# Eleven blocks of a transformer layer's weights by seven products of quarters, woven with the query/key tiles

## The chip, the core and the metric

The kernel runs on one core of one Trainium2 chip. The time is the device time of one execution, in microseconds (us). Engines are named as in the profile: PE is TensorE (PEld its weight loads), DVE is VectorE, ACT is ScalarE, POOL is GpSimd, SP is SyncE, which here only issues DMAs.

## What is computed

One layer on x of 256 tokens × 2048, in float32: a mixer with two branches, then a feed-forward block with a convolution over tokens. Each ends in a layer norm.

```
parts = x @ w_in                       # 2048 -> 9*1024 | 1024 1024 2048 2048 16 2048 2048
a_parts -> q, k, v of three dilated attention groups, 8 heads of 128
gq, gk, gv, gr, g_low, m_a, m_b = the rest
ya = (attention over the three groups) @ w_proj_a
o  = gated linear attention(gq, gk, gv, log_sigmoid(g_low @ gla_gate_w + b)/16)   # 4 heads, chunks of 64
yb = (rmsnorm(o) * silu(gr)) @ w_proj_b
y  = (sigmoid(m_a) * ya + sigmoid(m_b) * yb) @ w_out
x  = layernorm(alpha * x + y)
x  = layernorm(alpha * x + (silu(conv3(x @ w_gate)) * (x @ w_up)) @ w_down)
```

## The kernel before

All weights come as *pieces* of 128 partitions × 2048 float32 (1 MB), one DMA each on SP's queue, in the order of use. A piece is split in two parts that a single-pass matmul takes: `hi`, an ACT copy to float32r (L115), and `lo`, what is left, a DVE subtraction (L116). A product is then hi·hi + hi·lo + lo·hi. x is transposed and split in the same way, once (`X`, 16 blocks of 128 rows by 256 tokens, hi and lo side by side).

There are two forms of product. A *tile* (`b_tile`, L185 and L187) makes 128 output columns for all tokens, transposed: 16 matmuls of 512 with hi and 16 of 256 with lo. It serves q and k of the attention (48 tiles), gq and gk (16, `gqk`), gate and up of the feed-forward block (88, `fg` and `fu`). A *chunk* (`a_chunk`, L238 to L240) makes 512 output columns, with tokens on partitions: per piece 4 blocks of rows × 2 halves of tokens × 3 matmuls of 512, so 24 matmuls. It serves v, gv, gr, m, and the projections yp, pb, wo and wd.

The stages follow each other: v and q/k with the attention, gqk, gv, gr, then m, yp and pb in turn, wo, layer norm, the feed-forward block in parts of 20, 20 and 4 blocks (`FSPLIT`), the last norm. Small steps of attention and of the gated linear attention (GLA) are put in a list, `side`; `pump` takes one from it after a piece or a tile, so they stand between the products. One head of GLA is a chain: `gate` (pz, L483, then a log-sigmoid on ACT and DVE, L484 to L489), `decay` (a scan on DVE, L491, and exponentials), `keys` (q and k times these, L511, L517), `att` (ten small matmuls, L541, an ACT copy, a triangular mask on POOL, L549) and `outs` (pgo, L558 and L560, plain float32 matmuls, a root mean square and the output `o`, L567). Its four heads run beside the gv products.

Everything of the mixer stays in SBUF, in 38 buffers of 128x512 (`blk`). There are three buffers of raw pieces, two each of hi and lo, and 4 + 4 PSUM banks. The program's text is only a start for the order: a scheduler places the instructions of each engine, and the order on each engine is then fixed.

Of the kernel before, what the change touches and what calls it, by code (L numbers as in the profile page):

```python
# [20 lines left out]
NH = 8  # L21
# [14 lines left out]
FSPLIT = (20, 20, 4)  # L36
# [21 lines left out]
def hybrid_layer(ctx: ExitStack, tc: tile.TileContext, wp, xt, wgl, gw, par, relb, onehot, rows, xk, out):  # L58
    nc = tc.nc
    cpool = ctx.enter_context(tc.tile_pool(name="cpool", bufs=1))  # L60
    wpool = ctx.enter_context(tc.tile_pool(name="wpool", bufs=2))
    bpool = ctx.enter_context(tc.tile_pool(name="bpool", bufs=1))
    tpool = ctx.enter_context(tc.tile_pool(name="tpool", bufs=2))
    psm = ctx.enter_context(tc.tile_pool(name="psm", bufs=4, space=bass.MemoryType.PSUM))
    psx = ctx.enter_context(tc.tile_pool(name="psx", bufs=4, space=bass.MemoryType.PSUM))
    dpool = ctx.enter_context(tc.tile_pool(name="dpool", bufs=1, space=bass.MemoryType.DRAM))

# [11 lines left out]
    def blk(name, dt=F32):  # L79

        n_blk[0] += 1
        return bpool.tile([P, 512], dt, tag="blk", name=f"{name}_{n_blk[0]}", bufs=NBLK)

    def tmp(name, dt=F32):

        n_blk[0] += 1
        return tpool.tile([P, S], dt, tag="tmp", name=f"{name}_{n_blk[0]}", bufs=NTMP)

    def big(name, shape, dt=F32):

        n_blk[0] += 1
        return tpool.tile([P, *shape], dt, tag="big", name=f"{name}_{n_blk[0]}", bufs=7)

    def few(name, n, bufs=4):
        n_blk[0] += 1
        return tpool.tile([P, n], F32, tag=name, name=f"{name}_{n_blk[0]}", bufs=bufs)
# [15 lines left out]
    n_piece = [0]  # L112

    def split(hi, lo, src, engine=nc.vector):
        nc.scalar.activation(hi, src, AF.Copy)  # L115
        engine.tensor_tensor(lo, src, hi.bitcast(F32), op=ALU.subtract)  # L116

    def piece_in_blocks(i, on_pool=None):

        ws = []  # L120
        if on_pool is not None:
            raws = wpool.tile([P, 2048], F32, tag="raw", name=f"raw_{i}", bufs=3)
            nc.sync.dma_start(raws, wp[i])
        for c in range(4):
            cols = slice(c * 512, (c + 1) * 512)
            if on_pool is None:
                raw = blk("braw")
                nc.sync.dma_start(raw, wp[i, :, cols])
            else:
                raw = raws[:, cols]  # L130
            ws.append((blk("bhi", F32R), blk("blo", F32R)))
            split(*ws[-1], raw, nc.gpsimd if c in (on_pool or ()) else nc.vector)
        return ws

    def piece(before=(None,)):

        i = n_piece[0]
        n_piece[0] += 1
        raw = wpool.tile([P, 2048], F32, tag="raw", name=f"raw_{i}", bufs=3)
        hi = wpool.tile([P, 2048], F32R, tag="whi", name=f"whi_{i}")  # L140
        lo = wpool.tile([P, 2048], F32R, tag="wlo", name=f"wlo_{i}")
# [21 lines left out]
    def xtiles(name):  # L163
        return [bpool.tile([P, 4, 512], F32R, tag="xhl", name=f"{name}_{j}", bufs=4) for j in range(4)]

    X = xtiles("x")

    def load_x(j):
        def f():
            xr = blk("xraw")  # L170
            nc.sync.dma_start(xr, xt[:, j * 512 : (j + 1) * 512])
            k = slice(2 * (j % 2), 2 * (j % 2) + 2)
            xv = xr.rearrange("p (k t) -> p k t", k=2)
            split(X[j // 2][:, k, :S], X[j // 2][:, k, S:], xv)
        return f

# [13 lines left out]
    def b16(name, opnd, cuts=1):  # L190
        hi, lo = piece((None,) * cuts)
# [20 lines left out]
    def halves(a):  # L212
        return a.rearrange("p (a c) -> p a c", a=2)
# [557 lines left out]


NBLK = 38
NTMP = 12

# [114 lines left out]
```

## Time and profile before

| what | value |
|---|---|
| median of 3 runs | 1894.65 us (1894.32 to 1896.28) |
| the profiled execution's own time | 1894.34 us |
| span of that execution | 1892.5 us |
| PE / DVE / ACT / POOL busy | 99% / 58% / 46% / 4% |
| mean granted clock of PE | 0.997 |
| moved by DMA | 359.04 MB, 190 GB/s |

The span goes from the first to the last instruction that the profile shows; what lies outside it is start and end. Busy times of PE overlap a little, since matmuls are pipelined: how long a row of matmuls takes is read from the starts. The view of stages gives, for each stretch of the span, busy time and instruction count of PE, PEld, DVE, ACT and POOL, then the granted clock, the share of the 16 DMA engines and GB/s. In a timeline a row is start, duration, engine, line, operation, output and inputs, and in brackets the idle time before it and what ended that.

### The profile page before, as it was taken

How to read it: one execution, taken by the hardware profiler on the slowest of the kernel's cores; microseconds unless marked ns; L12 is line 12 of the kernel's file. 1: busy time of each engine (PE TensorE's matmuls, PEld its weight loads, DVE VectorE, ACT ScalarE, POOL GpSimd, SP SyncE). 2: the span in 40 equal slices, each digit the busy share in tenths (PEclk: the TensorE clock that was granted, in tenths of full speed). 3: DMA queues.
4: the chain of work that ended last, by engine and by line, in shares of the span. 5: the costliest groups of instructions: out<-in, count | busy, mean ns of one | idle time of the engine just before them, and what ended most of it. 6: DMA issues, size and time to landing. Idle time of an engine off the chain costs nothing.

```text
span 1892.5 us, 22845 instructions
## 1 busy us (share of the span) xinstructions
PE 1868.8 (99%) x9510; PEld 1585.6 (84%) x9510; DVE 1098.2 (58%) x1135; ACT 864.2 (46%) x936; POOL 81.0 (4%) x115
## 2 busy tenths in 40 slices
PE   8999999999999999999999999999999999999996
PEld 6888888888877788888888887888888888888885
DVE  5566475665655455445454557766644566664567
ACT  5445445454446544343434435555533455553342
POOL 0000000001000000000000003400000000000001
PEclk9999999999999999999999999999999999999998
DMA  8655545455534455555556654855555655555551
GB/s 283 237 178 180 193 167 193 172 189 181 182 137 155 150 184 181 197 193 187 198 182 219 236 195 145 242 203 190 191 180 198 245 185 194 184 194 185 215 200 67
DMA packets 57618, 359.04 MB, mean 190 GB/s; under 512 B 7089, under 2 KB 8012, under 8 KB 16940
## 3 DMA queue, kind: packets, MB, share of 16 engines
q1 hardware_dynamic: 52908, 345.10, 51.4%
q0 software_dynamic: 4464, 12.24, 2.5%
q8 instruction: 74, 1.21, 0.3%
q10 hardware_dynamic: 144, 0.26, 0.0%
q14 instruction: 28, 0.23, 0.0%
HBM read 355.41 MB, written 3.31 MB: 190 GB/s over the span
## 4 chain that ended last, share of the span: by engine, by line
PE 97%; DVE 2%; ACT 0%; issue 0%; DMA 0%; SPq 0%; ACTq 0%; DVEq 0%
PE qk L185 9%; PE fu L185 8%; PE fg L185 8%; PE qk L187 5%; PE fu L187 4%; PE fg L187 4%; PE wd_t L239 4%; PE wd_t L238 4%; PE wd_t L240 4%; PE gqk L185 3%; PE m_t L239 3%; PE m_t L240 3%; PE m_t L238 3%; PE v_t L238 2%; PE v_t L239 2%; PE v_t L240 2%
## 5 line engine op out<-in xcount | busy, mean ns | idle before, releaser
L116 DVE TENSOR_TENSOR wlo<-raw,whi 128x2048 fp32r<-128x2048 f32 (+1 forms) x336 | 738.8, 2201 | 662.3 <-ACT whi L115 645.7
L115 ACT ACTIVATE whi<-raw 128x2048 fp32r<-128x2048 f32 (+1 forms) x336 | 616.7, 1837 | 560.8 <-PE wd_t L240 107.9
L185 PE MATMUL qk<-x,whi 128*128 128x512 f32 x768 | 184.2, 392 | 0.0
L185 PEld LDWEIGHTS qk<-x,whi 128*128 128x128 f32 x768 | 140.9, 188 | 28.0
L185 PE MATMUL fu<-x,whi 128*128 128x512 f32 x688 | 164.3, 391 | 0.0
L185 PE MATMUL fg<-x,whi 128*128 128x512 f32 x672 | 160.2, 391 | 0.0
L185 PEld LDWEIGHTS fu<-x,whi 128*128 128x128 f32 x688 | 126.4, 188 | 24.5
L185 PEld LDWEIGHTS fg<-x,whi 128*128 128x128 f32 x672 | 123.6, 188 | 24.0
L238 PE MATMUL wd_t<-whi,h 128*128 128x512 f32 x344 | 133.9, 389 | 0.0
L239 PE MATMUL wd_t<-wlo,h 128*128 128x512 f32 x344 | 133.9, 389 | 0.0
L240 PE MATMUL wd_t<-whi,h 128*128 128x512 f32 x344 | 133.8, 389 | 0.0
L187 PEld LDWEIGHTS qk<-x,wlo 128*128 128x128 f32 x768 | 98.5, 191 | 3.8
L238 PE MATMUL m_t<-whi,x 128*128 128x512 f32 x256 | 99.9, 390 | 0.0
L187 PE MATMUL qk<-x,wlo 128*128 128x256 f32 x768 | 99.7, 283 | 0.0
L240 PE MATMUL m_t<-whi,x 128*128 128x512 f32 x256 | 99.6, 389 | 0.0
L239 PE MATMUL m_t<-wlo,x 128*128 128x512 f32 x256 | 99.6, 389 | 0.0
L187 PEld LDWEIGHTS fu<-x,wlo 128*128 128x128 f32 x688 | 88.2, 191 | 3.4
L187 PE MATMUL fu<-x,wlo 128*128 128x256 f32 x688 | 89.2, 283 | 0.0
L187 PEld LDWEIGHTS fg<-x,wlo 128*128 128x128 f32 x672 | 86.2, 191 | 3.3
L187 PE MATMUL fg<-x,wlo 128*128 128x256 f32 x672 | 87.2, 283 | 0.0
L238 PE MATMUL v_t<-whi,x 128*128 128x512 f32 x192 | 75.6, 396 | 1.7 <-ACT whi L115 1.7
L238 PEld LDWEIGHTS wd_t<-whi,h 128*128 128x128 f32 x344 | 64.6, 188 | 13.4
(229 smaller groups left out, 2717.7 us busy)
## 6 DMA issues: line engine op xcount, KB each, us to landing
raw<-in_wp SPq DMA_DIRECT2D x317, 1024.0 KB, 4.8
row<-in_rows POOLq DMA_DIRECT2D x24, 256.0 KB, 5.3
raw<-in_wp SPq DMA_DIRECT2D x20, 256.0 KB, 5.7
bias<-bvd POOLq DMA_DIRECT2D x32, 96.0 KB, 2.8
xraw<-in_xt SPq DMA_DIRECT2D x8, 256.0 KB, 5.7
r<-in_xk POOLq DMA_DIRECT2D x8, 256.0 KB, 5.3
braw<-in_wp SPq DMA_DIRECT2D x8, 256.0 KB, 6.0
out<-r SPq DMA_DIRECT2D x7, 256.0 KB, 2.5
```

The source lines that it names most:

```text
L115: nc.scalar.activation(hi, src, AF.Copy)
L116: engine.tensor_tensor(lo, src, hi.bitcast(F32), op=ALU.subtract)
L185: nc.tensor.matmul(ps, parts(kc)[0], opnd(kc), start=(kc == 0), stop=False)
L187: nc.tensor.matmul(ps[:, S:], parts(kc)[1], opnd(kc)[:, :S], start=False, stop=(kc == nk - 1))
L238: nc.tensor.matmul(ps, xh, hi, start=first, stop=False)
L239: nc.tensor.matmul(ps, xh, lo, start=False, stop=False)
L240: nc.tensor.matmul(ps, xl, hi, start=False, stop=last)
```

## The change

Eleven blocks of 2048 rows × 1024 columns (three of v, four of m, two of gv, two of gr) are no longer made by chunks. x and the block are cut in quarters, x by halves of tokens and of rows, the block by halves of rows and of columns; seven products of quarters (the form of Strassen and Winograd) give the four quarters of the result. `combine` makes four combinations of x once, on DVE. `seven` is one block, in seven steps: each product has two pieces of 12 matmuls. Four sums of weight pieces per block are made by DVE in place (`add`), four by a DMA on POOL's queue that adds into its destination (`add_by_dma`); five sums of results are made on DVE.

```
def part(ps, a, raw, p, first):
    hi, lo = two_parts(raw)
    for w, which in ((hi, 0), (hi, 1), (lo, 0)):
        for k in range(4): matmul(ps, a(4 * p + k)[which], w[:, k * 512 : (k + 1) * 512])
...
def add(a, b):
    tt(a, a, b, op=ALU.add)
def add_by_dma(a, b):
    nc.gpsimd.dma_start(a, b, accum_op=ALU.add)
...
def p1():      T = pieces 0, 1                     A = x11 T;  s = copy of A
def p5():      B12 = pieces 2, 3;  add(T, B12)     D = z T
def p67(p):    b = piece 4 + p;  add(T[p], b)      B += s2 T[p]
               add_by_dma(B12[p], b)               E += s3 B12[p]
               if p: s += B;  u = s + E;  store(1, 1, D - u)
def p3():      D += s4 B22;                        store(0, 1, D - s)
def p4():      B21 = pieces 6, 7;  add_by_dma(T, B21)   E = x22 T;  u += E;  store(1, 0, u)
def p2():      A += x12 B21;                       store(0, 0, copy of A)
```

(From `p1` on this is shortened; in the code each is a function of the names in `st`.)

The order of the work is new. The 16 gqk tiles come first, then the 48 of q and k, one after each of the 63 steps of nine blocks (v, m, gv):

```diff
-FSPLIT = (20, 20, 4)
+FSPLIT = (16, 16, 8, 4)
...
+    ratio = len(tiles) / len(steps)
+    done = 0
+    for n, step in enumerate(steps):
+        step()
+        pump()
+        while done < (n + 1) * ratio and tiles:
+            tiles.pop(0)()
+            done += 1
+            pump()
...
     for h in range(GH):
         stages, o = gla(h)
-        side.extend(stages)
-        GV.append(evacuate("gv", a_chunk("gv", xop, 16, n_pump=2)))
-        side.append(o)
+        side.extend([*stages, o])
+    for step in late:
+        step()
+        pump(2)
     drain()
+    early.close()
+    now[:] = ctx.enter_context(tc.tile_pool(name="late", bufs=1)), (17, 10, 1)
+    gbufs = []
...
-            raw = wpool.tile([P, 2048], F32, tag="raw", name=f"raw_{i}", bufs=3)
+    def raw_tile(i, tag="raw", bufs=2):
...
-                    nc.tensor.matmul(ps[:, : 2 * n], q[:, t * P : (t + 1) * P], halves(k)[:, :, :n], start=True, stop=False)
-                    nc.tensor.matmul(ps[:, n : 2 * n], q[:, S + t * P : S + (t + 1) * P], k[:, :n], start=False, stop=True)
+                    nc.tensor.matmul(pt, q[:, t * P : (t + 1) * P], k[:, :n], start=True, stop=True)
```

`late` holds the 14 steps of the two gr blocks; GLA's heads are pumped beside them, not beside gv. v, gqk, gv, gr, m, the attention's outputs and GLA's outputs are written to DRAM by POOL's queue (`spill`, L109) and read back when they are used (`fetch`, L114). When the early pool closes, a late pool takes its SBUF, and its first instructions are three memsets of `gbuf` (L736), then the fetches. After that come all four chunks of yp, all four of pb, and the rest as before. Attention's own matmuls take unsplit float32. Raw pieces have two buffers, hi three, and `quarter` six for the pieces that are summed. The pieces that were loaded in blocks ahead of time (first gate and up, last wd) are whole pieces now.

**Engine PE, in the stage that follows one head of GLA.** First the kernel before: the outputs of GLA's head 1 (`pgo`), the gate of the next (`pz`) and gv's products.

```order
L558 MATMUL pgo_540_5067<-gv_536_5031,att_535_4998 128x512 [waits Activation_49,Pool_49]
L558 MATMUL pgo_545_5077<-gv_536_5031,att_535_4998 128x512
L560 MATMUL pgo_545_5077<-gv_537_5033,att_535_4998 128x512 [waits Activation_49]
L483 MATMUL pz_550_5088<-glp_495_4663,gwp_492_4621 128x256
L238 MATMUL gv_t0_538_5035<-whi_97_5102,x_1_81 128x512 [waits Activation_49]
L239 MATMUL gv_t0_538_5035<-wlo_97_5103,x_1_81 128x512 [waits DVE_49]
```

Now the change, at the end of the second gr block: `grA` is its last product, `pgo_780` and `pgo_786` are head 1, `pz_792` to `pgo_818` head 2 (`patt` its scores); `pz_824` begins head 3.

```order
L308 MATMUL grA_712_6290<-wlo_797_6719,x_4_86 128x512 x3
L710 MATMUL pgo_780_6664<-gv_778_6660,att_774_6616 128x512 [waits DMASW0_49,Pool_49]
L710 MATMUL pgo_786_6676<-gv_778_6660,att_774_6616 128x512 [waits PE_49]
L712 MATMUL pgo_786_6676<-gv_779_6662,att_774_6616 128x512 [waits DMASW1_49]
L633 MATMUL pz_792_6689<-glp_661_5936,gwp_658_5894 128x256 [waits DVE_49]
L633 MATMUL pz_792_6689<-glp_661_5936,gwp_658_5894 128x256 [waits Activation_49]
L692 MATMUL patt_808_6763<-gq_803_6745,xk_805_6750 128x64 [waits DVE_49]
...
L710 MATMUL pgo_812_6781<-gv_810_6777,att_809_6774 128x512 [waits DMASW7_49,Pool_49]
L710 MATMUL pgo_818_6793<-gv_810_6777,att_809_6774 128x512 [waits PE_49]
L712 MATMUL pgo_818_6793<-gv_811_6779,att_809_6774 128x512 [waits DMASW0_49]
L633 MATMUL pz_824_6806<-glp_661_5936,gwp_658_5894 128x256 [waits DVE_49]
```

What moved: between the outputs of one head and the scores of the next stood products, and behind the last product there are now two whole heads with none.

**Engine POOL at the same place of the change** (before, only the mask stood there). `os` are the stores of GLA's outputs, `gq` and `gv` fetches for a head, `att` the mask, `yaf` fetches of the attention's outputs.

```order
L109 DMA os_785_6674<-o_784_6672 128x512 [waits DVE_49]
L109 DMA os_791_6687<-o_790_6685 128x512 [waits DVE_49]
...
L114 DMA gq_803_6745<-gkqs_140_1303 128x512 [waits DMASW5_49,DMASW1_49,PE_49]
L114 DMA gq_804_6747<-gkqs_84_654 128x512 [waits DMASW6_49,Pool_49]
L114 DMA gv_810_6777<-sp_649_5867 128x512 [waits DMASW7_49,DMASW2_49]
L700 AFFINE_SELECT att_809_6774<-att_809_6774 128x2x128 [waits Activation_49]
L114 DMA gv_811_6779<-sp_640_5782 128x512 [waits DMASW3_49,DMASW0_49]
...
L109 DMA os_851_6885<-o_850_6883 128x512 [waits DVE_49]
...
L114 DMA yaf_854_6899<-yas_248_2385 128x256
```

What moved: a head's q and k are fetched behind the stores of the head before, its second half of gv behind its own mask, and the attention's outputs behind the store of the last head.

**Engine DVE at the start of the change.** `wlo_54` is the low part of the third gqk tile, `comb` a combination of x (the last of four sets), `quarter` the two sums for step p5, `wlo_61` the low part of its first piece.

```order
L137 TENSOR_TENSOR wlo_54_355<-raw_2_352,whi_54_354 128x2048 [waits DMAHW3_49,PE_49]
...
L321 TENSOR_TENSOR quarter_64_308<-quarter_64_308,quarter_66_400 128x2048 [waits DMAHW4_49]
...
L321 TENSOR_TENSOR quarter_65_310<-quarter_65_310,quarter_67_402 128x2048 [waits DMAHW5_49]
L137 TENSOR_TENSOR comb1_25_241<-comb_45_293,comb1_25_241 128x2x128 [waits Activation_49]
L137 TENSOR_TENSOR comb2_26_242<-comb_46_294,comb2_26_242 128x2x128 [waits Activation_49]
L137 TENSOR_TENSOR comb3_27_243<-comb_47_295,comb3_27_243 128x2x128 [waits Activation_49]
L237 TENSOR_TENSOR gqk_56_391<-gqk_55_358,pa_57_392 128x256 [waits Activation_49]
...
L137 TENSOR_TENSOR wlo_61_408<-quarter_64_308,whi_61_407 128x2048
```

What moved: before, only the splits of x and of the first pieces stood at the start of DVE's row; now both sums and all combinations stand ahead of p5's first low part.

596 lines of the change are left out of this document (360 added, 236 removed).

## The prediction

> **What bounds the kernel now.** I read the page first: the busy times, the chain that ended last and the clock row. The three lines show TensorE (PE) busy for 99% of the span, on 97% of the chain, and at full granted clock.
>
> ```profile
> PE 1868.8 (99%) x9510; PEld 1585.6 (84%) x9510; DVE 1098.2 (58%) x1135; ACT 864.2 (46%) x936; POOL 81.0 (4%) x115
> ...
> PEclk9999999999999999999999999999999999999998
> ...
> PE 97%; DVE 2%; ACT 0%; issue 0%; DMA 0%; SPq 0%; ACTq 0%; DVEq 0%
> ```
>
> So a PE instruction that goes saves its pitch, as long as no other engine becomes later than PE. Next, the busy time by stage: the columns are PE, PEld, DVE, ACT, POOL, then clock, DMA share and GB/s.
>
> ```profile
> 0.00:10.00 10.00, 5.19 (x9) 1.62 (x10) 1.44 (x3) 2.54 (x3) 2.80 (x15) 1.00 0.69 197
> 10.00:75.00 65.00, 65.00 (x284) 53.71 (x283) 39.09 (x38) 33.16 (x35) 4.38 (x8) 1.00 0.80 284
> ...
> 534.00:646.00 112.00, 111.67 (x521) 87.29 (x520) 62.47 (x72) 62.79 (x100) 1.63 (x4) 1.00 0.42 147
> 646.00:739.00 93.00, 93.00 (x418) 76.09 (x417) 49.09 (x37) 41.83 (x40) 0.00 (x0) 1.00 0.50 175
> ```
>
> The third row is the stage of GLA (the gated recurrence) beside the gv products, the fourth the gr products. In both PE has no hole, while DVE is about half idle. GLA is a long chain of small steps, and here it is free because PE has products to do meanwhile. Busy times of PE overlap, so I take pitches from starts. A block piece (24 matmuls of 512) takes the period of the ACT copies in the wd products, 1407.98 − 1402.54 = 5.44 us, .227 per matmul; a query/key-like tile takes half of 1191.54 − 1180.41, 5.57 us.
>
> ```profile
> 1402.54 1.92 ACT L115 ACTIVATE whi<-raw 128x2048 fp32r<-128x2048 f32 x1 [3.52 <-PE wd_t L240]
> 1407.98 1.92 ACT L115 ACTIVATE whi<-raw 128x2048 fp32r<-128x2048 f32 x1 [3.52 <-PE wd_t L240]
> ```
> ```profile
> 1180.41 3.82 PE L185 MATMUL fg<-x,whi 128*128 128x512 f32 x16
> ...
> 1191.54 3.82 PE L185 MATMUL fg<-x,whi 128*128 128x512 f32 x16
> ```
> ```profile
> 1135.05 3.60 PE L673 MATMUL keep<-r,ones 128*128 128x512 f32 x8
> ```
>
> The last row is four plain F32 matmuls in 3.60 us: .90 each, four times a single-pass one.
>
> **The products.** A 2048×1024 block took 2 × 4 pieces × 24 = 192 matmuls; seven products of quarters take 7 × 24 = 168. Eleven blocks: 11 × 24 × .227 = −60 us. Attention now uses F32 matmuls instead of split ones. Per head and group, scores went over 256 + 128 + 512 + 256 = 1152 columns at .227 per 512 (.51 us) and go over 384 at .90 (.68 us); the mix likewise. 24 × 2 × .17 = +8 us. PE's own work falls by 52 us.
>
> **The weight sums in the middle.** A block now has 14 splits instead of 8, four sums of 128x2048 on DVE and five adds of 128x512.
>
> ```profile
> L116 DVE TENSOR_TENSOR wlo<-raw,whi 128x2048 fp32r<-128x2048 f32 x316 | 725.6, 2296 | 656.8 <-ACT whi L115 640.3 <-ACT pa L230 9.5 <-PE ps L337 4.1
> L115 ACT ACTIVATE whi<-raw 128x2048 fp32r<-128x2048 f32 x316 | 604.6, 1913 | 553.2 <-PE wd_t L240 107.9 <-PE m_t L240 85.3 <-PE gqk L185 46.0
> ...
> L608 DVE TENSOR_TENSOR sg<-sg,gr_t 128x512 f32<-128x512 f32 x8 | 5.5, 688 | 4.7 <-ACT sg L607 4.6
> ...
> L517 DVE TENSOR_TENSOR xk<-gqk,ga 128x256 f32<-128x256 f32 x8 | 3.0, 419 | 0.0
> ```
>
> DVE: 18 × 2.296 + 5 × .688 = 44.8 us against 7 × 5.44 = 38.1 of PE. But nine blocks have 64 tiles beside them, 7.1 each: PE 38.1 + 7.1 × 5.57 + some 6 of attention = 84; DVE 44.8 + 7.1 × (2.296 + .42) + 5 = 69; ACT about 14 × 1.913 + 7.1 × 2.3 + 5 = 48. PE still ends last, and these sums cost nothing there: its tiles cover them. The two sums by DMA have one to two steps (a product and a tile, 11 to 12 us) between issue and use.
>
> ```profile
> raw<-in_wp SPq DMA_DIRECT2D x317, 1024.0 KB, 4.8
> row<-in_rows POOLq DMA_DIRECT2D x24, 256.0 KB, 5.3
> ...
> bias<-bvd POOLq DMA_DIRECT2D x32, 96.0 KB, 2.8
> ```
> ```profile
> q1 hardware_dynamic: 52908, 345.10, 51.4%
> ```
>
> No row shows an accumulating DMA. From below it is a 1 MB load, 4.8 us; from above, 256 KB on POOL's queue in 5.3, scaled by four, 21. I take about 8: the load row, plus 1892.5 × .514 / 345.1 = 2.8 us of all 16 engines for a second reading of 1 MB. It is nearest to that row, same bytes and layout. Hidden: 0; both ends are kept for a rival. DMA share per block: 15 loads and 4 double moves, 23 × 2.8 = 65 of 84 us, not a bound.
>
> **The start.** It costs +13 us (5 to 18). These rows are the first split on DVE, and the first matmuls.
>
> ```profile
> 6.83 0.69 DVE L116 TENSOR_TENSOR x<-xraw,x 128x512 fp32r<-128x512 f32 x1 [5.89 <-ACT x L115]
> ```
> ```profile
> 8.80 1.22 PE L238 MATMUL v_t<-whi,x 128*128 128x512 f32 x2 [1.71 <-ACT whi L115]
> ...
> 12.55 0.39 PE L238 MATMUL v_t<-whi,x 128*128 128x512 f32 x1
> 12.78 0.39 PE L239 MATMUL v_t<-wlo,x 128*128 128x512 f32 x1
> ```
>
> Before, PE loses 8.8 us and then runs at half pace until 12.55 (9 matmuls of .227 in 3.75): 10.5 in all. Now the first tile needs all of x, 2 MB, and 1 MB of weights: 3 MB at 284 GB/s after a first landing is about 17 us. Then DVE has, ahead of p5's first low part, seven instructions of 128x2048 (that low part included), 32 of 128x256 for the combinations of x and three for tiles: 16.1 + 13.4 + 1.3 = 31, so it is done at 48. PE's work until there is three tiles, p1 and two thirds of a piece, 24 us: it loses 24 where it lost 10.5. The ends: DVE has part of this done before x is complete, or the loads come later than that rate. No later slack returns it.
>
> **The gr blocks.** These two have no tiles beside them, only GLA. DVE 2 × 44.8 = 89.6 and half of GLA's vector work, some 13; PE 76.2 + 12. DVE is now the later by 14; what it has done ahead (two low parts, 4.6) comes off: +10 us (5 to 18).
>
> **GLA's last heads run bare.** The order has heads 2 and 3 behind the last gr product with no product between, and yp waits for data fetched behind them. Here is the chain of one head, as it ran under gv: first ACT, then DVE, POOL.
>
> ```profile
> 553.52 0.63 ACT L486 ACTIVATE ga<-gz 128x512 f32<-128x512 f32 x1
> ...
> 554.85 0.72 ACT L488 ACTIVATE ga<-ga,one 128x512 f32<-128x512 f32 x1
> ...
> 567.10 0.49 ACT L547 ACTIVATE att<-patt 128x384 f32<-128x384 f32 x1 [2.23 <-PE patt L541]
> ...
> 572.24 0.58 ACT L562 ACTIVATE sq<-pgo 128x512 f32<-128x512 f32 x1
> ```
> ```profile
> 555.60 0.69 DVE L489 SCALAR_TENSOR_TENSOR gz<-gz,ga 128x512 f32<-128x512 f32 x1 [0.15 <-ACT ga L488]
> 556.33 1.22 DVE L491 TENSOR_TENSOR_SCAN gc<-rmask,gz 128x512 f32<-128x512 f32 x1
> ...
> 561.63 0.69 DVE L511 SCALAR_TENSOR_TENSOR gqk<-gqk,ge 128x512 f32<-128x512 f32 x1
> 562.23 0.76 DVE L517 TENSOR_TENSOR xk<-gqk,ga 128x256 f32<-128x256 f32 x2
> 562.90 0.69 DVE L517 TENSOR_TENSOR xk<-gqk,gz 128x128 f32<-128x128 f32 x3
> ...
> 574.57 0.74 DVE L567 SCALAR_TENSOR_TENSOR o<-pgo,rs,NG 128x512 f32<-128x512 f32 x1
> ```
> ```profile
> 567.66 0.41 POOL L549 TENSOR_SCALAR_AFFINE_SELECT att<-att 128x256 f32<-128x256 f32 x1 [57.06 <-ACT att L547]
> ```
>
> One head bare: pz and its copies 1; three activations 2.0; gz and scan 1.9; exponent or difference .7; keys .69 + .76 + .69 and .6 of small steps, 2.7; patt 1.8; att and select .9; then POOL's issue (.6) and the gv half's fetch, 5.3 as the 256 KB row; pgo 2.7; some 14 hand-overs, 1. Sum 20.6. PE's own part, 5.3 (pgo 2.7, patt 1.8, pz .8), is in the count already: 15.3 idle. The q and k fetches stand on POOL behind the stores of the head before, which wait for its output: 2.5 for that, two issues and 5.3 end 3 us after the chain wants them. 2 × 18.5 = 37. The end of head 1, whose select is placed 8 matmuls before the last product ends: 3.5. From head 3's pgo to yp: norm 2.0 (.58, two tiny activations, .74), store 3.4, fetch 3.4 to 5.9, split .8: 10.5. PE's slow restart, by the start's rows: 2. Together **+53 us** (34 with every fetch at 2.8 as the bias row, nothing queued, no hand-overs and no slow restart: 2 × 11.8 + 1 + 9.6; 65 with 5.3 everywhere, 6 of queueing a head and PE's own part a half longer: 2 × 21.3 + 3.5 + 12.1 + 2 + 5).
>
> [...] The rows at 8.80 to 12.55 agree with half pace after idling; no row shows it for a gap in the middle.
>
> **The rest.** Two raw buffers instead of three: DVE's split ends at 1303.16 + 2.29 = 1305.45, a load of 4.8 lands at 1310.3.
>
> ```profile
> 1303.16 2.29 DVE L116 TENSOR_TENSOR wlo<-raw,whi 128x2048 fp32r<-128x2048 f32 x1 [1.08 <-ACT whi L115]
> ```
> ```profile
> 1312.35 1.91 ACT L115 ACTIVATE whi<-raw 128x2048 fp32r<-128x2048 f32 x1
> ```
>
> The second piece on wants it at 1312.35, so 2 us of cover: 0, and if that cover is gone, what the load is late. Whole pieces at FFN's start and in the last wd instead of prefetched blocks: +2 (0 to 8).
>
> **Sum.** −52 + 13 + 10 + 53 + 2 = +26: span 1892.5 + 26 = 1918.5. The profiled execution took 1894.34, 1.8 outside the span (and .3 below the median of the three): **1920 us**, +1.4%. With low ends, −52 + 5 + 5 + 34 = −8; with high ends, −52 + 18 + 18 + 65 + 8 = +57.
>
> **The rivals.**
> *A short bare stretch (faster).* Place: between the last gr product and the first yp matmul; mechanism: its DMA hops (q and k, gv, store, fetch) land in 2.8 instead of 5.3 and queue behind nothing, so it costs 34. For it: 96 KB in 2.8. Against it: 256 KB in 5.3, and POOL's stores stand ahead. With start and gr at their low ends, 1894 − 8 = 1886. It makes the kernel faster below 38 us of bare stretch with these ends, below 23 with my values. 0.15.
> *Slow sums by DMA.* An accumulate of 1 MB takes 21 us, 9 more than the step that covers it; two pairs per block, each pair once late, make 18 more in eleven blocks, ~200 at worst; at half of it +100, 2018. For it: 5.3 for 256 KB on this queue. Against it: 4.8 for 1 MB of the same layout. It decides at about 12 us, in the gr blocks at 5 to 7. 0.10.
> *Loads bind the FFN.* With two buffers a load later by .25 us than its 2 us cover on 200 pieces gives +50: 1968. Against it: the median load of 4.8 would have to become 7. 0.05.
> Forecast: 0.70.
>
> **How the numbers follow.** About 0.2% (4 us) is what a measurement of this kernel can tell from no change. Faster: the short stretch 0.15 and a little of the forecast's lower end, 0.17. Same: a stretch of 34 to 40 with one of start and gr above its low end, 0.07. Slower: 0.76. Range: 1886 to 1960, from the short stretch to the high ends (1951) and a little of the loads' case; left out are most of the slow sums and what lies below the low ends. The likeliest case alone: 1902 to 1942.
>
> **What would show it.** Right: PE idle about 24 us up to p5's first low matmul; no waits of PE for POOL's queue in the middle blocks; in gr, PE waiting for low parts by about 5 us a block; some 60 us from the last gr product to yp with PE nearly idle; FFN stages as before. Wrong: a bare stretch below 38 us with PE hole-free else, or waits for sums by DMA in the middle stage, or FFN pieces late for their loads.

## The result, and the profile after

The changed kernel takes 1985.19 us (median of four runs, 1983.73 to 1987.01), the kernel before 1895.1 beside it: 1.0475 times as long, 95% interval 1.0457 to 1.0493. The sign was forecast, the size was not: 1920 was predicted, and 1985 lies above the range. The profiled execution took 1983.73 us, its span is 1981.9.

First the page of the changed kernel, with the parts that were read of the kernel before, and rows for what the change adds: the queue of GpSimd, DVE's sums of weight pieces, and the DMA issues.

```profile
PE 1859.2 (94%) x9246; PEld 1558.7 (79%) x9246; DVE 1333.7 (67%) x1181; ACT 974.6 (49%) x951; POOL 203.2 (10%) x305
...
PEclk9989999999999999887699999999999999999998
...
q0 software_dynamic: 21360, 91.95, 18.9%
...
PE 82%; DMA 6%; DVE 6%; issue 3%; ACT 2%; POOL 1%; SPq 0%; ACTq 0%; POOLq 0%; DVEq 0%
...
L321 DVE TENSOR_TENSOR quarter<-quarter,quarter 128x2048 f32<-128x2048 f32 x44 | 100.4, 2286 | 0.7
...
raw<-in_wp SPq DMA_DIRECT2D x235, 1024.0 KB, 5.0
...
quarter<-quarter POOLq DMA_DIRECT2D x44, 1024.0 KB, 8.5
```

PE held 97% of the chain before and holds 82% now; DMA and DVE, which took 2% together, take 6% each. The median accumulate, 8.5 us, is what the prediction took (8). So neither PE's work nor the usual price of a sum by DMA explains the result: something waits at particular places. The windows show where (PE, PEld, DVE, ACT, POOL, then clock, DMA share, GB/s).

```profile
0.00:60.00 60.00, 43.33 (x188) 32.11 (x189) 46.82 (x63) 32.13 (x43) 3.97 (x12) 0.94 0.88 295
60.00:130.00 70.00, 53.51 (x253) 44.30 (x252) 38.82 (x26) 30.87 (x21) 7.44 (x12) 0.88 0.70 223
130.00:782.00 652.00, 651.25 (x3348) 554.42 (x3347) 521.19 (x381) 364.97 (x293) 83.17 (x126) 1.00 0.86 272
782.00:917.00 135.00, 114.14 (x462) 87.84 (x462) 102.09 (x87) 73.60 (x78) 24.87 (x42) 0.87 0.66 185
917.00:984.00 67.00, 30.17 (x77) 18.15 (x76) 21.86 (x38) 24.98 (x59) 20.88 (x36) 0.59 0.34 117
1208.00:1280.00 72.00, 57.31 (x286) 44.68 (x284) 52.79 (x59) 33.51 (x46) 33.61 (x31) 0.91 0.52 168
```

PE is full for 652 us in the middle, and in no other row. Busy time hides half pace (eight matmuls are 3.78 us of it at 841.21 and 1.97 at 797.73), so the account below takes starts: of each matmul the distance to the next start, less the usual distance for that line and shape. The surplus is called *lost*. What is left is PE's own work: 1847.8 us before, 1795.3 after, −52.5. The usual distance is a choice: with medians of undisturbed rows the own work falls by 56, and what a row of the table has more than before moves by up to 3.

| stretch of the changed kernel | lost before / after, us | more lost | predicted |
|---|---|---|---|
| start, 0 to 60 | 3.6 / 19.0 | 15 | 13 |
| end of the first v block, 60 to 130 | 0 / 19.9 | 20 | 0 |
| middle blocks, 130 to 782 | 13.0 / 12.7 | 0 | 0 |
| gr blocks, 782 to 917 | 1 / 39.1 | 38 | 10 |
| bare heads to yp, 917 to 984 | 0 / 50.5 | 50 | 53 |
| yp to wo, 984 to 1208 | | 3 | 0 |
| norm and start of the FFN, 1208 to 1280 | 4.9 / 21.2 | 16 | 2 |
| sum | | 143 | 78 |

143 − 52.5, and 1 less behind the last matmul, is the span's +89.4. Three rows are wrong: the first block, gr, and the start of the FFN.

**The first block.** Timelines of the changed kernel: PE, then ACT, then POOL, from 79 to 113 us.

```profile
90.47 2.07 PE L214 MATMUL gqk<-x,wlo 128*128 128x256 f32 x16
107.19 3.79 PE L308 MATMUL vE<-whi,x 128*128 128x512 f32 x8 [14.65 <-ACT whi L136]
```
```profile
105.22 1.91 ACT L136 ACTIVATE whi<-quarter 128x2048 fp32r<-128x2048 f32 x1 [21.46 <-DMA quarter<-quarter]
...
112.31 1.91 ACT L136 ACTIVATE whi<-quarter 128x2048 fp32r<-128x2048 f32 x1 [4.91 <-DMA quarter<-quarter]
```
```profile
79.90 0.57 POOL L546 DMA_DIRECT2D vs<-c  x1 [17.68 <-DVE c L358]
84.56 0.54 POOL L109 DMA_DIRECT2D gkqs<-gqk  x1 [4.09 <-DVE gqk L237]
88.03 0.54 POOL L546 DMA_DIRECT2D vs<-s  x1 [2.92 <-DVE s L364]
88.61 2.20 POOL L430 DMA_DIRECT2D bias<-bvd  x4
90.80 1.90 POOL L324 DMA_DIRECT2D quarter<-quarter  x2
```

Step p4 (`vE` with x22) is ready for PE at 92.5. Its first sum lands at 105.2, because its accumulate is issued only at 90.80 and then takes 14.3 us; the second takes 20.8. Ahead of them POOL stood three times at the store of a result that DVE had not finished. The bracket of 90.80 names no wait, so when the sums' own inputs were there can't be read here; an experiment tells.

**The gr blocks.** PE of the changed kernel at two of seven holes, then ACT at the second, then POOL's issue of the accumulate that ACT waits for.

```profile
797.73 1.97 PE L308 MATMUL grD<-whi,comb 128*128 128x512 f32 x8
803.61 2.08 PE L308 MATMUL grD<-wlo,comb 128*128 128x512 f32 x4 [3.91 <-DVE wlo L137]
...
841.21 3.78 PE L308 MATMUL grE<-whi,x 128*128 128x512 f32 x8 [4.38 <-ACT whi L136]
```
```profile
839.25 3.71 ACT L136 ACTIVATE whi<-quarter 128x2048 fp32r<-128x2048 f32 x2 [4.35 <-DMA quarter<-quarter]
```
```profile
825.65 0.88 POOL L324 DMA_DIRECT2D quarter<-quarter  x1 [1.44 <-DMA quarter<-in_wp]
```

The first hole waits for a low part of DVE, as predicted, the other for ACT's copy of a piece that was summed by DMA. That accumulate was issued at 825.65, when its own input had landed, and took 13.5 us. By what ended them, the seven holes are 6.9 us behind such copies (two holes), 5.4 behind DVE's low parts (two), 3.2 behind a sum of results on DVE, 2.6 behind GLA's keys and 1.4 behind the fetch of a gv. Behind the five holes of 2.55 to 4.38 us PE is slow: eight matmuls take 3.78 us at 841.21, where the granted clock is .50 (841.21 to 844.8), and the eight at 797.73, ahead of the holes, take 1.97. By starts the seven holes cost 20.6 us in all, and the slow matmuls behind them at least 12 of the other 18.

**The bare heads.** PE of the changed kernel from gr's last matmuls on.

```profile
916.72 1.08 PE L308 MATMUL grA<-wlo,x 128*128 128x512 f32 x4
921.20 2.81 PE L710 MATMUL pgo<-gv,att 128*128 128x512 f32 x4 [3.41 <-POOL att L700]
926.88 2.08 PE L712 MATMUL pgo<-gv,att 128*128 128x512 f32 x2 [2.86 <-DMA gv<-sp]
...
941.51 1.97 PE L692 MATMUL patt<-gq,xk 128*128 128x64 f32 x8 [10.22 <-DVE xk L668]
...
961.39 1.97 PE L692 MATMUL patt<-gq,xk 128*128 128x64 f32 x8 [6.72 <-DVE xk L668]
...
979.75 0.80 PE L244 MATMUL yp_t<-whi,ya 128*128 128x512 f32 x1 [8.42 <-ACT ya L136]
```

A head takes 961.39 − 941.51 = 19.9 us, where its chain was priced at 20.6 and the lateness of its q and k at 3 more; the select of head 1 costs 3.4 (3.5 was said), the hand-over to yp 8.4 (10.5).

**The start of the FFN.** Groups of DVE from 1224 to 1262 us: number, busy us, mean ns.

```profile
L137 DVE TENSOR_TENSOR wlo<-raw,whi 128x2048 fp32r<-128x2048 f32 x4 | 13.2, 3291 | 5.2 <-PE fg L231 4.4 <-ACT whi L136 0.8
L869 DVE TENSOR_TENSOR x<-x1f,x 128x512 fp32r<-128x512 f32 x6 | 6.8, 1159 | 0.2 <-ACT x L866 0.2
L864 DVE TENSOR_SCALAR x1f<-pt,prm 128x256 f32<-128x256 f32 x8 | 4.0, 535 | 0.3 <-PE pt L861 0.2
```

A low part takes 3.29 us here, where 2.29 is usual. In the same window POOL multiplies r by its gate rows and adds; below that, the same work in the kernel before (1150 to 1225).

```profile
L877 POOL TENSOR_TENSOR r<-r,row 128x512 f32<-128x512 f32 x8 | 13.6, 1698 | 1.2 <-DMA row<-in_rows 1.1
```
```profile
L702 POOL TENSOR_TENSOR r<-r,row 128x512 f32<-128x512 f32 x8 | 12.6, 1570 | 29.4 <-DMA row<-in_rows 29.4
```

The same instructions, but before they were spread out by 29.4 us of waiting for their rows; now the rows are there, and they run dense beside DVE's low parts. Whether that costs the 16 us, or the order and the buffers do, needed a test.

### The profile page after: what moved, and what is told of

It reads as the page before. It is cut to its first block, busy times and chain, and to the rows that moved or that the text cites. A ratio compares the mean times of both kernels' runs of the same rounds, so it can differ in the third digit from the quotient of the medians.

```text
span 1981.9 us, 23097 instructions
## 1 busy us (share of the span) xinstructions
PE 1859.2 (94%) x9246; PEld 1558.7 (79%) x9246; DVE 1333.7 (67%) x1181; ACT 974.6 (49%) x951; POOL 203.2 (10%) x305
## 3 DMA queue, kind: packets, MB, share of 16 engines
q0 software_dynamic: 21360, 91.95, 18.9%
## 4 chain that ended last, share of the span: by engine, by line
PE 82%; DMA 6%; DVE 6%; issue 3%; ACT 2%; POOL 1%; SPq 0%; ACTq 0%; POOLq 0%; DVEq 0%
PE qk L212 8%; PE fu L212 8%; PE fg L212 8%; PE qk L214 4%; PE fu L214 4%; PE fg L214 4%; PE wd_t L244 4%; PE wd_t L246 4%; PE wd_t L245 4%; DMA quarter<-quarter 3%; PE mA L308 2%; PE gqk L212 2%; DVE wlo L137 2%; PE mD L308 2%; PE mE L308 2%
## 5 line engine op out<-in xcount | busy, mean ns | idle before, releaser
L136 ACT ACTIVATE whi<-raw 128x2048 fp32r<-128x2048 f32 (+1 forms) x239 | 452.7, 1894 | 502.1 <-DMA raw<-in_wp 381.3
L137 DVE TENSOR_TENSOR wlo<-raw,whi 128x2048 fp32r<-128x2048 f32 (+1 forms) x239 | 544.7, 2279 | 213.2 <-PE wd_t L245 52.3
L137 DVE TENSOR_TENSOR wlo<-quarter,whi 128x2048 fp32r<-128x2048 f32 x154 | 351.8, 2287 | 151.5 <-ACT whi L136 125.2
L136 ACT ACTIVATE whi<-quarter 128x2048 fp32r<-128x2048 f32 x154 | 294.2, 1917 | 233.3 <-DMA quarter<-quarter 79.2
L212 PE MATMUL qk<-x,whi 128*128 128x512 f32 x768 | 188.6, 396 | 0.0
L244 PE MATMUL wd_t<-whi,h 128*128 128x512 f32 x352 | 137.1, 390 | 0.0
L246 PE MATMUL wd_t<-whi,h 128*128 128x512 f32 x352 | 136.9, 389 | 0.0
L321 DVE TENSOR_TENSOR quarter<-quarter,quarter 128x2048 f32<-128x2048 f32 x44 | 100.4, 2286 | 0.7
L246 PEld LDWEIGHTS wd_t<-whi,h 128*128 128x128 f32 x352 | 66.1, 188 | 14.0 <-DVE h L137 0.2
L244 PEld LDWEIGHTS wd_t<-whi,h 128*128 128x128 f32 x352 | 66.1, 188 | 13.8 <-ACT h L136 0.5
```

What stands on the lines that cost most here:

```text
L137: nc.vector.tensor_tensor(lo, src, hi.bitcast(F32), op=ALU.subtract)
L212: nc.tensor.matmul(ps, parts(kc)[0], opnd(kc), start=(kc == 0), stop=False)
L244: nc.tensor.matmul(ps, xh, hi, start=first, stop=False)
L246: nc.tensor.matmul(ps, xl, hi, start=False, stop=last)
L321: tt(a, a, b, op=ALU.add)
```

## The experiments

All are edits of the changed kernel (1985 us). Ratios are to the kernel before, on the same chip.

### The sums by DMA

**No sums by DMA.** Four of eight weight sums per block are left out.

```diff
-            nc.gpsimd.dma_start(a, b, accum_op=ALU.add)
+            pass
```

> The changed kernel (1985 us) with the 44 accumulating DMAs left out, so the products that use these sums read unsummed weights. Its order at the end of gr differs a little (one of the last two GLA heads gets some products beside it). Theory A, as predicted: the accumulates are covered by a step everywhere, and gr is late through DVE's low parts; then only the order's difference shows, 1965 to 1985 us, and the wait of 15 us near 92 us in the first block stays. Theory B: the accumulates stand in POOL's queue behind stores that wait for results, and come late in the first block (20 us with the slow clock behind it) and in gr (10 to 11 us of waits for pieces summed by DMA, 8 of slow clock behind them); then 20 us go before 130 us, some 18 in gr, and the time is 1930 to 1950.

1951.85 us, ratio 1.0302 (1.0267 to 1.0337), 2 us above what the theory of late sums expects, and far below the other. The loss in 60 to 130 falls from 19.9 us to under 1, and from the first gr product to yp it takes 179.7 us instead of 197.2. The sums by DMA cost some 33 us, nearly all of it in these two places.

**All sums on DVE.**

```diff
-            nc.gpsimd.dma_start(a, b, accum_op=ALU.add)
+            add(a, b)
```

> The changed kernel with all 88 weight sums on DVE, none by DMA. Theory B (late accumulates, and what stands behind them in the in-order queues of ACT and POOL): the 20 us before 130 us go; the middle is still covered (DVE 54 + 24 of 84 us a block); gr has DVE later by 2 x 9.2 us, but loses the waits for sums (19 with the slow clock); 1960 to 1975 us. Rival: DVE becomes the bound of the middle blocks, 3 to 5 us each, and of gr: 1995 to 2020.

1961.89 us, ratio 1.0352 (1.0308 to 1.0397), as expected: 23 us less, though DVE does 44 × 2.29 = 101 us more. The loss in 60 to 130 is 4, the middle is as it was, and from the first gr product to yp it takes 189.2 us instead of 197.2, 8 less. In the middle blocks either engine's sums are free; in the first block and in gr the DMA's are the dearer.

**The stores on SyncE's queue.** That the place in POOL's queue makes the sums late is one theory, their own transfer time the other.

```diff
-            nc.gpsimd.dma_start(VS[g][n][:, t], c)
+            nc.sync.dma_start(VS[g][n][:, t], c)
...
-            table[2 * u + n][t] = spill("sp", c)
+            n_blk[0] += 1
+            d = table[2 * u + n][t] = dpool.tile(list(c.shape), F32, name=f"sp_{n_blk[0]}")
+            nc.sync.dma_start(d, c)
```

> The changed kernel, with one edit: the stores of the seven-product results are issued by SyncE and no longer by GpSimd, so that no store that waits for VectorE stands ahead of the accumulating DMAs on GpSimd's queue (the four bias transfers still do). Queue theory (the accumulates are late because of where they stand): the first block's accumulate is issued at about 80 us and not at 90.8, most of the 20 us lost in 60-130 go and a little in the gr blocks: 1955 to 1970 us. Rival (the accumulates' own 14 to 21 us of transfer decide, or SyncE's loads are now held up behind the stores): no gain, 1983 us or more.

1992.4 us, ratio 1.0515 (1.0484 to 1.0546). POOL in this run:

```profile
97.63 0.97 POOL L324 DMA_DIRECT2D quarter<-quarter  x1 [10.71 <-DMA quarter<-in_wp]
```

The accumulate comes later still, because now it waits for its own input: SyncE stood at the stores at 79.22 and 87.35, and its loads of quarters, issued from 66.22 on in the changed kernel, start at 88.24. The wait had only moved to the other queue, so this run says nothing on the transfer time.

**The stores on ScalarE's queue**: the four of the first v block and the eight of the gqk tiles; SyncE's loads stay as they were.

```diff
-        nc.gpsimd.dma_start(d, src)
+        e = nc.scalar if name == "gkqs" and n_blk[0] < 700 else nc.gpsimd
+        e.dma_start(d, src)
...
-            nc.gpsimd.dma_start(VS[g][n][:, t], c)
+            (nc.gpsimd if g else nc.scalar).dma_start(VS[g][n][:, t], c)
```

> The changed kernel, with one edit: in the first v block the four result stores, and the stores of the first query/key products, are issued by ScalarE's queue and not by GpSimd's, so that on GpSimd only the bias transfers stand ahead of the two accumulating DMAs of p4, and SyncE's loads stay as they are. Queue theory (the accumulates' sources have landed by about 82 us, and only GpSimd's queue holds them to 90.8): they are issued at 80 to 84 us, land 8 or more us before 105.1 and 112.2, and the 19.9 us lost in 60-130 fall by 8 to 16: 1969 to 1977 us. Rival (the transfer itself, 14 to 21 us, or a late source decides): they are issued at 88 us or later, or land as late as before; 1982 us or more.

1971.81 us, ratio 1.0408 (1.036 to 1.0455). POOL, then PE, of this run:

```profile
64.72 2.26 POOL L431 DMA_DIRECT2D bias<-bvd  x4 [15.98 <-DMA bvd<-bvs]
75.69 0.94 POOL L325 DMA_DIRECT2D quarter<-quarter  x1 [8.71 <-DMA quarter<-in_wp]
78.20 0.87 POOL L325 DMA_DIRECT2D quarter<-quarter  x1 [1.57 <-DMA quarter<-in_wp]
```
```profile
95.45 2.08 PE L215 MATMUL gqk<-x,wlo 128*128 128x256 f32 x16
97.37 2.00 PE L309 MATMUL vE<-whi,x 128*128 128x512 f32 x8
```

The accumulates go out as soon as their inputs land, 15 us earlier, take 12.0 and 15.1 us, and PE reaches `vE` without a wait. 5.1 us are lost in 60 to 130 instead of 19.9, and those are PE's 3.15 behind ACT, which now holds the store, and slow matmuls after it (16 in 5.55 us at 90.07, where the 16 at 75.75 take 3.79). So in the first block it was the queue. The transfers of 12.0 and 15.1 us, issued at 75.69 and 78.20, do no harm here.

### The gr blocks and the bare heads

**Five side steps per gr step**, so that GLA is done before the products end.

```diff
-        pump(2)
+        pump(5)
```

> The changed kernel with five side steps instead of two taken after each step of the gr blocks, so GLA's chains start earlier and no head stands behind the last product. Theory A: the 50 us from the last gr product to yp are GLA's chain without cover; with products behind the heads it falls to 10 to 20 and the time to 1945 to 1960 us. Theory B: PE's order is fixed, so it waits for the same chains in the middle of gr (two heads there still have few products between their steps); the waits move forward and the time stays within 1970 to 1985.

1993.24 us, ratio 1.052 (1.049 to 1.0551): no gain, and above both ranges. As theory B says, the heads now wait inside gr, up to 18.2 us at `patt` for DVE's keys. Without more products beside them, earlier steps only move the waits.

**Tiles over eleven blocks.**

```diff
-    ratio = len(tiles) / len(steps)
+    ratio = len(tiles) / (len(steps) + len(late) - 6)
...
-    for step in late:
+    for n, step in enumerate(late, len(steps)):
...
+        while done < (n + 1) * ratio and tiles:
+            tiles.pop(0)()
+            done += 1
+            pump()
```

> The changed kernel with the 64 tiles spread over all eleven blocks (until six steps before the end) instead of nine, GLA's steps at the front of the side list of gr. Theory A: gr gets cover for DVE, for the sums by DMA and for GLA: gr's loss of 39 us falls to about 10, the bare stretch of 50 to 20, and the first block stays: 1920 to 1940 us. Theory B: with 5.8 tiles a block instead of 7.1 PE has 76 us for DVE's 64 and one step less cover for POOL's queue, so the middle begins to wait for sums: 5 us a block, 1960 to 1975.

1975.36 us, ratio 1.0426 (1.0384 to 1.0468): 10 less, at the upper end of theory B. Both theories hold in part: from the first gr product to yp 23 us less are lost, ahead of gr (130 to 760) some 11 more. The worst hole left is 16.0 us at `patt`, and ACT's timeline shows where half of it comes from.

```profile
893.63 0.63 ACT L637 ACTIVATE ga<-ga 128x512 f32<-128x512 f32 x1
900.77 1.91 ACT L136 ACTIVATE whi<-quarter 128x2048 fp32r<-128x2048 f32 x1 [6.51 <-DMA quarter<-quarter]
902.58 0.70 ACT L638 ACTIVATE ga<-ga,one 128x512 f32<-128x512 f32 x1
```

The input of GLA's logarithm (L638) was ready at 894.26, but it stands on ACT behind a copy that waits for an accumulate, and starts 8.3 us later. So this late sum cost what it held up on ACT too, not only its own product.

**GLA beside the m blocks.** gv right after v, GLA's steps among the m blocks, the tiles spread over all blocks.

```diff
-    ratio = len(tiles) / len(steps)
...
-    for step in late:
+    steps = steps[:21] + steps[49:63] + steps[21:49] + late
+    ratio = len(tiles) / (len(steps) - 6)
+    done = 0
+    for n, step in enumerate(steps):
+        if n == 35:
+            set_up()
         step()
-        pump(2)
+        pump(2 if n >= 35 else 1)
```

(`set_up` holds GLA, its preparation and its steps, which stood behind the loop over the other blocks.)

> The changed kernel with the two gv blocks right behind v, GLA's steps in the side list from then on (beside the m blocks and their tiles), gr last, and the tiles spread until six steps before the end; the sums by DMA stay. Theory A: GLA's chains are then under products for good: the bare stretch of 50 us falls to the hand-over to yp, about 12, and gr has tiles as cover; the first block's 20 us stay. 1920 to 1940 us. Rival: PE's order is fixed and waits for a chain wherever it stands, as in the run pump_five: 1965 to 1985.

1956.34 us, ratio 1.0323 (1.0278 to 1.0367), between the two expectations: 29 less. Of the bare stretch only the hand-over to yp is left (10.4 us), but some 35 us more are lost between 400 and 625, beside m. Of the 22 us of holes there 11 are ahead of GLA's own matmuls and 4 ahead of a product that waits behind a step of GLA on ACT; the rest are waits of attention and of the products themselves.

**The same, with DVE's sums in the first v block and in gr.**

```diff
-            nc.gpsimd.dma_start(a, b, accum_op=ALU.add)
+            if name in ('gr',) or (name == "v" and i == AT["v", 0]):
+                add(a, b)
+            else:
+                nc.gpsimd.dma_start(a, b, accum_op=ALU.add)
```

> The same as gla_beside_m, with the sums of the first v block and of the gr blocks on DVE instead of by DMA. Theory B: the waits for late accumulates in those places go as well, 20 us in the first block and some 5 to 10 in gr: 1890 to 1915 us, near the kernel before. Rival: the accumulates are late at other places then, or DVE is late in gr: within 10 us of gla_beside_m.

1942.30 us, ratio 1.0249 (1.0176 to 1.0322); more was expected. The first block's loss is gone (4 left), the others stay: some 35 beside m, the hand-over, the FFN's 23.

### The start

**Five tiles ahead of the first block**, not two.

```diff
+    tiles.pop(0)()
+    tiles.pop(0)()
+    tiles.pop(0)()
```

> The changed kernel with five tiles ahead of the first seven-product block instead of two. Theory, as predicted: PE waits 24 us at the start because DVE makes the combinations of x and two sums ahead of p5's first low part; with 17 us more of PE's own work there, and 8 of DVE's, 7 to 10 us go before 60 us. The rest of the order moves too: GLA's heads by a little; 1970 to 1980 us. Rival: the combinations move back with the tiles; the start stays as it is, 1983 to 1987.

1987.21 us, ratio 1.0489 (1.0468 to 1.051): no gain. The scheduler put DVE's combinations of x later by as much, and the waits came back behind the tiles. So the place of the tiles alone does not help; that the work of DVE ahead of p5 decides the start is argued from its order, since no run makes that work less.

### The start of the FFN

Two theories: POOL's products beside DVE's low parts, or the order and the buffers.

**Eight empty side steps ahead of POOL's products.**

```diff
+    side.extend([lambda: None] * 8)
```

> The changed kernel with the eight scalings of the residual on POOL taken up eight feed-forward blocks later; nothing else moves. Theory B: POOL's 128x512 products stretch the DVE instructions beside them (a 128x2048 low part took 3.0 to 4.7 us there, 2.3 elsewhere), and this is the loss at the start of the feed-forward block (21 us against 5 before); 8 to 14 us go, 1971 to 1977 us. Theory A: the loss comes from whole pieces in place of blocks loaded ahead, and from two raw buffers; no change, 1983 to 1987.

1984.39 us, ratio 1.0474 (1.0443 to 1.0504). The trace has POOL's products at 1224 to 1261, as without the edit, so it tells nothing.

**The same, and the side steps held behind an instruction of the FFN.**

```diff
+    side.extend([lambda: None] * 8)
...
-            pump()
+            with tc.issue_after(gated.ins):
+                pump()
```

> The changed kernel with the scalings of the residual on POOL really held back to feed-forward blocks 8 to 15 (in the run gain_later the scheduler had left them where they were). Theory B: POOL beside DVE stretches DVE's instructions, and this is the loss at the start of the feed-forward block (21 us); 8 to 14 us go, 1971 to 1977 us, and the low parts there take 2.3 us again. Theory A: the loss comes from whole pieces and two raw buffers: 1983 to 1987.

1985.43 us, ratio 1.0476 (1.0431 to 1.0521). The products again ran at 1226 to 1261: inconclusive as well.

**Second and third pieces of the FFN's first blocks in buffers of their own.**

```diff
-        ws = [by_cols(piece(i)) for i in idx]
+        def apart(i, *tag):
+            raw = load(i, *tag)
+            n_blk[0] += 2
+            hi, lo = (wpool.tile([P, 2048], F32R, tag="quarter", name=f"q{k}_{n_blk[0]}", bufs=6) for k in range(2))
+            split(hi, lo, raw)
+            return hi, lo
+
+        ws = [by_cols(piece(idx[0])), by_cols(apart(idx[1])), by_cols(apart(idx[2], "quarter", 6))]
```

> The changed kernel with the second and third piece of the feed-forward block's start split into buffers of their own (the six that the sums used, free by then), instead of the two for low parts. Theory: the loss of 21 us there is that the third low part and the next pieces wait until the first low part has been used; 10 to 16 us go, 1969 to 1975 us. Rival: the raw pieces come late or the layer norm holds PE; within 4 us of 1985.

1987.29 us, ratio 1.0489 (1.0468 to 1.051). From the last wo product to the first wd it takes 209.0 us, 207.0 without the edit: these buffers are not the cause.

**POOL's products made to wait for a result of a later block**, by a small copy into their rows' buffers.

```diff
+    def row_after(i, n):
+        b = blk("row")
+        nc.gpsimd.tensor_copy(b[:, :1], seen[-1][:, :1])
+        return row(i, n, b)
...
-            nc.gpsimd.tensor_tensor(a, a, row(2, n), op=ALU.mult)
-            nc.gpsimd.tensor_tensor(a, a, row(3, n), op=ALU.add)
+            nc.gpsimd.tensor_tensor(a, a, row_after(2, n), op=ALU.mult)
+            nc.gpsimd.tensor_tensor(a, a, row_after(3, n), op=ALU.add)
...
+    side.extend([lambda: None] * 8)
...
+            seen.append(sg)
```

> The changed kernel, with one edit: the buffers in which GpSimd holds the gate rows r scaled for the FFN blocks first get a small copy that depends on a result of a later block, so the row products of GpSimd (1.3 to 2.8 us each) cannot run in 1224-1261 us, where they stand beside the low parts of VectorE in the changed kernel. Theory B (GpSimd's products stretch VectorE's low parts there from 2.29 us to 3 to 4.7 us, and TensorE runs dry): the low parts take about 2.3 us, the 16 us lost at the start of the FFN fall by 8 to 14, 1971 to 1977 us. Theory A (the order of VectorE's queue, or the buffers, makes the loss): the gaps stay, 1983 to 1987 us.

1975.93 us, ratio 1.0428 (1.0398 to 1.0458). The same groups of DVE in this run, 1226 to 1264:

```profile
L137 DVE TENSOR_TENSOR wlo<-raw,whi 128x2048 fp32r<-128x2048 f32 x6 | 13.7, 2288 | 8.5 <-PE fg L231 4.9 <-ACT whi L136 2.9 <-PE fu L214 0.7
L864 DVE TENSOR_SCALAR x1f<-pt,prm 128x256 f32<-128x256 f32 x9 | 4.6, 538 | 1.9 <-PE pt L861 1.8
L869 DVE TENSOR_TENSOR x<-x1f,x 128x512 fp32r<-128x512 f32 x6 | 3.9, 684 | 0.2 <-ACT x L866 0.2
```

With POOL quiet, a low part takes 2.29 us instead of 3.29 and L869 takes .68 instead of 1.16; L864, which reads PSUM, is the same in both. POOL has no instruction from 1205 to 1290 in this run. From the last wo product to the first wd it takes 195.7 us instead of 207.0, 11 less, and the kernel's time falls by 9: the products beside DVE made 9 to 11 of the 16.

### A smaller change

**Seven products for v and m alone**: gv and gr as chunks again, GLA beside gv, all sums on DVE, the tiles beside v and m.

```diff
-            nc.gpsimd.dma_start(a, b, accum_op=ALU.add)
+            add(a, b)
...
-    ratio = len(tiles) / len(steps)
+    n_tiles = len(tiles)
+    due = lambda n: 0.95 * n if n <= 21 else 20 + (n_tiles - 20) * (n - 21) / (len(steps) - 21)
...
+        keep_in(GV[h], "gv", a_chunk("gv", xop, 16, AT["gv"] + 4 * h, n_pump=2))
...
+        keep_in(GR[h], "gr", a_chunk("gr", xop, 16, AT["gr"] + 4 * h, n_pump=2))
```

> Seven products only for v and m (seven blocks), the weight sums all on DVE; gv and gr by chunks as before the change, with GLA's steps beside them; the 64 tiles over the 49 steps of seven blocks; stores, fetches and the feed-forward block as in the changed kernel. Theory: PE's work falls by 38 - 8 = 30 us; the start costs 15, the hand-over to yp 10, the feed-forward start 16, the rest nothing, since every block of seven has 9 tiles as cover (PE 97 us, DVE 86) and no GLA head is bare: 1900 to 1918 us. Rival: DVE or POOL's stores are late in the middle with all sums on DVE: 1925 to 1950.

1929.76 us, ratio 1.0185 (1.0165 to 1.0206): in the rival's range, but not for its reason, since 130 to 682 loses only 3 us. The bare heads are gone; lost are still 19 us at the start, some 31 from the first gv product to yp (8 of them the hand-over to yp, 8 at `patt`) and some 23 at the FFN.

**The same with five tiles first and the FFN's pieces apart.**

```diff
+    tiles.pop(0)()
+    tiles.pop(0)()
+    tiles.pop(0)()
...
+    due = lambda n: 0.8 * n if n <= 21 else 17 + (n_tiles - 17) * (n - 21) / (len(steps) - 21)
...
+        ws = [by_cols(piece(idx[0])), by_cols(apart(idx[1])), by_cols(apart(idx[2], "quarter", 6))]
```

> seven_only_v_m with five tiles ahead of the first block, and the parts of the feed-forward start in buffers of their own. Theory: the two repairs add up, 8 and 12 us: 1880 to 1898 us, near or below the kernel before. Rival: each repair only moves its wait: within 6 us of seven_only_v_m.

1937.32 us, ratio 1.0232 (1.0214 to 1.0249): worse. The start loses 6 us less and the first block 12 more; repairs that bring nothing alone bring nothing together.

**Seven products for v and m, with POOL's products made to wait**, the edit shown above.

```diff
-            nc.gpsimd.tensor_tensor(a, a, row(2, n), op=ALU.mult)
+            nc.gpsimd.tensor_tensor(a, a, row_after(2, n), op=ALU.mult)
```

> seven_only_v_m (1929.76 us) with the edit of gain_waits. If GpSimd's row products beside VectorE's low parts make the loss at the start of the FFN: 1915 to 1922 us. If they don't: 1928 to 1932 us.

1923.17 us, ratio 1.015 (1.012 to 1.0179), between the two ranges and near the first. From the last wo product to the first wd 12 us go here too; 5 of them are lost again between the first gr product and yp. It is the fastest version of the study, and still 1.5% above the kernel before.

## Why the prediction was wrong

The losses came to 143 us and not 78. Of the 65 that were missed 20 are the first block, 28 gr and 14 the start of the FFN.

- **"PE's own work falls by 52 us"**: right, 52.5.
- **"It costs +13 us" (the start)**: right, 15. p5's first low part was priced to be done at 48; it stands on DVE at 47.27, as the first of a row of two, and ends at 49.5.
- **"PE still ends last, and these sums cost nothing there" (the middle)**: right: 0 more is lost in 652 us, with the accumulates at 7 to 14 us.
- **"The two sums by DMA have one to two steps ... between issue and use ... Hidden: 0"**: this step failed. It counted the cover from the place in the program and took the issue to come as early. DVE's work in between was added up, the order on POOL's queue in the first block was not: a store that waits for DVE stands ahead of the accumulates there. That made them 15 us late; with the stores on another queue the 15 us came back. Their own 14 and 21 us are more than the 8 taken too, but issued early, 12 and 15 did no harm.
- **"+10 us (5 to 18)" (gr)**: the mechanism was half of it. PE does wait for DVE's low parts; its low parts and one sum of results make 8.6 us of holes, near the 10. The term left out the waits for accumulates (6.9), those for GLA's keys and gv (4.0), and the slow matmuls behind the holes (12 or more). Lost: 38. The causes were not separated to the last us: with DVE's sums 8 us come back from gr and the heads together, with the sums left out 18, and the rest stays.
- **"Slow sums by DMA ... It decides at about 12 us, in the gr blocks at 5 to 7"**: this rival held, in the first block and in gr and no other place. It was given 0.10, because its price was asked of the transfer (8 or 21 us) and not of the issue. For the first block the late issue is shown as the cause; in gr the accumulate behind the longest such hole waited last for its own input and then took 13.5 us, and no run tells which of the two decides there.
- **"Together +53 us" (bare heads)**: right, 50, with errors that cancel. PE's clock there is .59 and its own part of a head is about 10 us (941.51 to 946.05, 947.10 to 951.60 and a pz of .9), not 5.3; the gv fetch is in time for heads 2 and 3. The small matmuls take twice as long there: behind a gap of 10.22 us the eight at 941.51 take 1.97 us at a granted clock of .50 (941 to 947), where the eight at 915.35 took 1.00. No row of before had shown this for a gap in the middle; in gr one of 2.55 us had it, ahead of 824.09. The sum, which took them at full pace but for a slow restart of 2, came out all the same.
- **"Whole pieces at FFN's start ... +2 (0 to 8)"**: the term looked at the loads. What got worse is DVE, by POOL's products that the change packs together: 16 us, 9 to 11 of them shown by the run that makes them wait.

## What to carry to other kernels

Where a transfer is issued from a queue that also issues stores of results, its cover is counted from the moment the last store ahead of it can go (the accumulate of the first block went at 90.80 us, and at 75.69 with the stores on another queue), so read that queue in order before you call a transfer hidden. Moving the stores to another queue helps only if nothing needed soon stands behind them there: on ScalarE's queue it gave 13 us, on SyncE's, ahead of the loads, it cost 7. And a hole in PE can cost more than its length: the one of 2.55 us ahead of 824.09 cost 2 to 3 us more, since 12 matmuls of gr behind it stood .42 us apart or more and not .227. A late input on ACT can hold up what is queued behind it, as it did GLA's logarithm by 8.3 us.

## What the runs showed of the hardware

- A 1 MB accumulate from SBUF to SBUF lands 7.0 to 20.8 us after its issue, 8.5 in the median. The queue that carries them, with the other DMAs of POOL, takes 1981.9 × .189 / 91.95 = 4.07 us of all 16 engines per MB; the plain loads of the kernel before took 2.8.
- A hole of 2.55 us (ahead of 824.09 in gr) had slow matmuls behind it: the granted clock was .50 from 824 to 828, and the matmuls stood .43 us apart where .227 is usual, for some 8 to 14 of them behind the holes of 2.55 to 4.38 us in gr, then full pace. A single hole of 2.02 us had no such effect: the clock was 1.00 from 1251.5 to 1256. Two holes of 1.83 and 1.95 us with two small matmuls between them had it (.50 from 1216.4 to 1220). PE of the changed kernel:

```profile
824.09 0.79 PE L308 MATMUL grE<-whi,x 128*128 128x512 f32 x1 [2.55 <-ACT whi L136]
...
825.96 3.62 PE L308 MATMUL grD<-whi,comb 128*128 128x512 f32 x8
...
1251.51 3.93 PE L212 MATMUL fg<-x,whi 128*128 128x512 f32 x16 [2.02 <-ACT whi L136]
```

- While GpSimd multiplied (1224 to 1262 of the changed kernel), two groups of VectorE with both inputs in SBUF were stretched against the run that makes GpSimd wait: a low part from 2.29 to 3.29 us in the mean, L869 from .68 to 1.16. L864, which reads PSUM, was not (.535 and .538). The four low parts took 3.16, 3.04, 2.29 and 4.68 us; beside the third, at 1251.49, it was GpSimd's product that took longer, 3.06 us at 1251.86, where 12 of the 16 took 1.28 to 1.31.
